# Half-width block products and a spread-out unit order in the feed-forward part of a two-layer encoder trunk

## The chip, the cores and the metric

The kernel runs on one core of one Trainium2 chip. The metric is the time of one execution in microseconds (us) on the device. TensorE (PE) multiplies matrices, VectorE (DVE) and ScalarE (ACT) work element by element, GpSimd (POOL) and SyncE (SP) issue transfers here. Each engine takes its own instructions strictly in the order in which the program lists them for it.

## The reference

Two layers, 256 tokens, width 2048. Each layer is a combined projection, an attention group and a retention group, an output projection, a layer norm, a SwiGLU feed-forward part of width 5632, and a second layer norm. What the change touches is the feed-forward part:

```python
D_MODEL, SEQ, DEPTH, D_FF = 2048, 256, 2, 5632
for l in range(DEPTH):
    ...
    x = layer_norm(ALPHA * x + mix, ln1_g[l], ln1_b[l])
    f = (jax.nn.silu(x @ w_gate[l]) * (x @ w_up[l])) @ w_down[l]
    x = layer_norm(ALPHA * x + f, ln2_g[l], ln2_b[l])
```

All inputs and the output are float32.

## The kernel before

**Units.** All weights reach the chip as blocks of 1 MB (128 partitions x 2048 float32). A list made at build time, `UNITS`, gives the order in which the kernel consumes them, one *unit* at a time. Each unit is prepared in `Weights._prep`: its block is loaded (`raw`), ScalarE rounds it to a high part (`hi`, the cast of L288) and VectorE subtracts to get the low part (`lo`, L289). TensorE then makes three matmuls for each piece: high weights by high activations, low by high, high by low. Three pairs of `hi`/`lo` buffers go round, so that unit number i can be prepared only when TensorE has finished unit i-3; until then the unit has no buffer. Loads are asked for up to four units ahead. This is the heart of `_prep` for a Strassen unit:

```python
if frm is not None and kind not in by_dma:
    V.tensor_tensor(r[into], r[into], r[frm], ALU.add)
split(hi[:, o:o + 2048], lo[:, o:o + 2048], r[into])
```

`split` is the cast and the subtraction. Plain ("std") blocks have long been split in two halves of 1024 columns, a cast and a subtraction each; Strassen units are split in one piece of 2048.

**The feed-forward part.** The first 512 columns of gate and up are computed plainly. The other ten column groups pair the gate and the up projection in a Strassen-Winograd scheme over four weight blocks 11, 12, 21, 22. It needs seven products: B11, B21 and B22 use a block as it is; T1 uses 11+12, T2 uses 11+12+22, T3 uses 12+22, and T4 takes 21 in as well. Here the sums are made in place in `raw`. Most are VectorE additions (L220): T1 and T2 in every group, T3 in half groups too. T4, and T3 in full groups, get their sum by a transfer that POOL issues and that adds into `raw` as it lands (`ADD_BY_DMA`, L225).

**Groups.** A *half* group (`HALF_ORDER`) works on 512 columns and half the depth; four plain units (sg1, sg3, su1, su3) do the rest of the depth. A *full* step is two groups of 256 columns at full depth, and blocks of the down projection (D, `down`) are put between their products (`FULL_ORDER`: four D in a group, or two in the last step). Per layer there are five half groups, eight full groups with four D, and two with two D, in the order half, full, full, half, full, full, and so on; behind them stand the last eight D. In each of the ten Strassen steps, `flush` turns the hidden values of the step before (eight transposes on TensorE, two casts and two subtractions) at a fixed position in the first group.

**Names in rows.** `raw`, `hi`, `lo` are the weight tiles; `sX`, `sY`, `sZ`, `sW`, `sQ`, `sR` are PSUM banks: sX takes B11 and then B21, sW takes T1 and then B22, sY takes T2, sZ takes T3, sQ takes T4, and sX, sQ, sR, sW also take the plain units of a half group; `db` is the bank of a D, `pth` that of the transposes, `v` are the running vectors. L895 is the copy of the B11 result, L916 to L918 finish T4. The build's scheduler arranges each engine's instructions by its own estimate of readiness, so an engine's order can differ from the written one.

Of the kernel before, what the change touches and what calls it, by code (L numbers as in the profile page):

```python
# [13 lines left out]
AF = mybir.ActivationFunctionType  # L14
ALU = mybir.AluOpType
# [5 lines left out]
D = 2048  # L21
# [4 lines left out]
HR = 4  # L26
FF = 5632
NFF = FF // 512
HALF_ORDER = ("B11", "T1", "sg1", "T2", "B21", "sg3", "T3", "su1", "B22", "su3", "T4")
FULL_ORDER = {4: ("B11", "T1", "T2", "D", "B21", "D", "T3", "D", "B22", "D", "T4"),  # L30
              2: ("B11", "T1", "T2", "B21", "D", "T3", "B22", "D", "T4")}
FF_STEPS = [("half", 1, ())]
for _f in (2, 4, 6, 8):
    FF_STEPS += [("full", _f, tuple((n, (_f - 2, _f - 1)) for n in range(4))), ("half", _f + 1, ())]
# [17 lines left out]
def weight_plan():  # L52
# [15 lines left out]
    def strassen(l, c, half=None):  # L68
        rows, nk, c0, ncol = (1024, 4, 512 * c, 512) if half is None else (1024, 8, 512 * c + 256 * half, 256)
        return {i: add("w_gate" if i[1] == "1" else "w_up", l, rows * (int(i[0]) - 1), nk, c0, ncol)  # L70
                for i in ("11", "12", "22", "21")}

    for l in range(DEPTH):
# [28 lines left out]
        for mode, c, groups in FF_STEPS:  # L102
            if mode == "half":
                b = strassen(l, c)
                for kind in HALF_ORDER:
                    if kind[0] == "s":
# [3 lines left out]
            else:  # L110
                todo = [(n, cc) for n, cs in groups for cc in cs]
                per = len(todo) // 2
                for half in range(2):
                    b = strassen(l, c, half)
                    for kind in FULL_ORDER[per]:
                        if kind == "D":
# [12 lines left out]
def shift(b):  # L129
    name, _, _, _, c0, ncol = PLAN[b]  # L130
    if name in ("w_gate", "w_up") and ncol == 256:
        return 48
    if name == "w_in" and ncol == 128 or name in ("w_uq", "w_ukv") and c0 < 1024:
        return 16
    return 0
# [9 lines left out]
def trunk(ctx: ExitStack, tc: tile.TileContext, x, pos, w, lnp, cols, eye, consts, out):  # L145
    nc = tc.nc
    V, A, PE, G = nc.vector, nc.scalar, nc.tensor, nc.gpsimd
# [21 lines left out]
    def bank(tag_name):  # L169
        return psp.tile([P, 512], F32, tag="ps", name=tag_name)  # L170

    class Weights:
# [26 lines left out]
        def _prep(self):  # L199
            i = self.n_prep  # L200
            if i >= len(UNITS):
                return
            self.loads(i + 1)
            hi = wspl.tile([P, W_SPL], F32R, tag="hi", name=f"hi{i}")
            lo = wspl.tile([P, W_SPL], F32R, tag="lo", name=f"lo{i}")
            kind, b = UNITS[i]
            if kind == "std":
                n = SIZES[b]
                raw = self.raw.pop(b)
                o = shift(b)  # L210
                for a, e in ((0, n // 2), (n // 2, n)):
                    split(hi[:, o + a:o + e], lo[:, o + a:o + e], raw[:, a:e])
            else:
                r = {j: self.raw.get(b[j]) for j in b}
                ncol, o = PLAN[b["11"]][5], shift(b["11"])
                by_dma = ADD_BY_DMA[ncol]
                into, frm = {"B11": ("11", None), "B21": ("21", None), "B22": ("22", None), "T1": ("11", "12"),
                             "T2": ("11", "22"), "T4": ("11", "21"), "T3": ("12", "22")}[kind]
                if frm is not None and kind not in by_dma:
                    V.tensor_tensor(r[into], r[into], r[frm], ALU.add)  # L220
                split(hi[:, o:o + 2048], lo[:, o:o + 2048], r[into])
                nxt = {"T1": ("T3", "12", "22"), "T2": ("T4", "11", "21")}.get(kind)
                if nxt is not None and nxt[0] in by_dma:
                    j = b[nxt[2]]
                    G.dma_start(r[nxt[1]], w[OFFS[j]:OFFS[j + 1]].rearrange("(p n) -> p n", p=P), accum_op=ALU.add)  # L225
                for j in {"T4": ("11",), "T3": ("12",), "B22": ("22",), "B21": ("21",)}.get(kind, ()):
                    self.raw.pop(b[j])
            self.hi[i], self.lo[i] = hi, lo
            self.n_prep += 1
            self.loads(i + 4)  # L230
# [56 lines left out]
    def split(hi, lo, src):  # L287
        A.copy(hi, src)  # L288
        V.tensor_tensor(lo, src, hi.bitcast(F32), ALU.subtract)  # L289

    def rsqrt(v, n):
        r = small.tile([P, 4], F32, tag="rs", name="rs")
        G.tensor_tensor(r[:, :n], v, mhalf[:, :n], ALU.pow)
        return r
# [164 lines left out]
    for l in range(DEPTH):  # L459
# [22 lines left out]
        for t in range(2):  # L482
# [7 lines left out]
            r = rsqrt(v, 2)  # L490
# [373 lines left out]
        def xs(t, k0, nk):  # L864
            ts = slice(t * P, (t + 1) * P)
            return (xTh[:, k0:k0 + nk, ts], xTl[:, k0:k0 + nk, ts])

        def mm(ps, unit, st, first=False):
            wh, wl = unit
            nk = st[0].shape[1]  # L870
            for k in range(nk):
                a, b = st[0][:, k, :], st[1][:, k, :]
                PE.matmul(ps, a, wh[:, k, :], start=first and k == 0, stop=False, skip_group_check=True)  # L873
                PE.matmul(ps, a, wl[:, k, :], start=False, stop=False, skip_group_check=True)  # L874
                PE.matmul(ps, b, wh[:, k, :], start=False, stop=k == nk - 1, skip_group_check=True)  # L875

        def strassen_group(order, nk, ncol, c0, v, downs):
            v2, v3, v5, sg = (t[:, c0:c0 + ncol] for t in v)
            s1, s2, s3, s4 = ((sfh[:, i, :nk], sfl[:, i, :nk]) for i in range(4))
            B = {}  # L880

            def acc(name, unit, st):
                new = name not in B
                if new:
                    B[name] = bank("s" + name)[:, :ncol]
                mm(B[name], unit, st, new)

            for i, kind in enumerate(order):
                if kind == "D":
                    next(downs)()  # L890
                    continue
                (unit,) = W.get()
                if kind == "B11":
                    acc("X", unit, xs(0, 0, nk))
                    A.copy(v2, B["X"])  # L895
                elif kind == "T1":
                    acc("W", unit, s1)
                elif kind == "T2":
                    acc("Y", unit, s2)
                    V.tensor_tensor(v2, B["Y"], v2, ALU.subtract)  # L900
                elif kind == "B21":
                    acc("X", unit, xs(0, 8, nk))
                    if "sg3" not in order:
                        A.activation(sg, B["X"], AF.Silu)
                elif kind == "T3":
                    acc("Z", unit, s3)
                    V.tensor_tensor(v3, B["Z"], v2, ALU.add)
                    V.tensor_tensor(v5, B["W"], v3, ALU.add)
                elif kind == "B22":
                    acc("W", unit, s4)  # L910
                    if "su3" not in order:
                        V.tensor_tensor(v2, B["W"], v2, ALU.add)
                        V.tensor_tensor(v2, v2, sg, ALU.mult)
                elif kind == "T4":
                    acc("Q", unit, xs(1, 8, nk))
                    V.tensor_tensor(v3, B["Q"], v3, ALU.subtract)  # L916
                    A.activation(v3, v3, AF.Silu)
                    V.tensor_tensor(v5, v5, v3, ALU.mult)  # L918
                elif kind in ("sg1", "sg3"):
                    acc("X", unit, xs(0, 4 * int(kind[2]), 4))  # L920
                    if kind == "sg3":
                        A.activation(sg, B["X"], AF.Silu)
                    acc("Q", unit, xs(1, 4 * int(kind[2]), 4))
                else:
                    acc("R", unit, xs(1, 4 * int(kind[2]), 4))
                    if kind == "su3":
                        V.tensor_tensor(v5, B["R"], v5, ALU.add)
                    acc("W", unit, xs(0, 4 * int(kind[2]), 4))
                    if kind == "su3":
                        V.tensor_tensor(v2, B["W"], v2, ALU.add)  # L930
                        V.tensor_tensor(v2, v2, sg, ALU.mult)
                W.done()
                if i == 1:
                    flush()

        plain_group()
        for mode, c, groups in FF_STEPS:
            v = [vt512(n) for n in ("v2", "v3", "v5", "sg")]
            if mode == "half":
                strassen_group(HALF_ORDER, 4, 512, 0, v, None)  # L940
            else:
                downs = down_list(groups)
                per = sum(len(cs) for _, cs in groups) // 2
                for half in range(2):
                    strassen_group(FULL_ORDER[per], 8, 256, 256 * half, v, downs)
            hprev.append((c, (v[0], v[2])))
# [124 lines left out]
```

## Time and profile before

| | before |
|---|---|
| median of 3 runs | 2330.65 us (2329.36 to 2331.11) |
| the profiled execution | 2328.0 us, span 2326.2 us |
| PE busy | 2208.3 us, 95% of the span, 12676 matmuls |
| DVE busy | 1696.3 us, 73% |
| ACT busy | 1082.2 us, 47% |
| mean granted clock of TensorE | 0.983 |
| HBM traffic | 202 GB/s over the span |

The span runs from the first to the last instruction of the profiled execution; the time of that execution is a little longer. The ends of matmuls are modelled, so a busy PE is not a PE at its peak; what a stretch costs is better read from the starts of matmuls.

### The profile page before, as it was taken

The numbers are of one execution on the slowest core, as the hardware profiler recorded it, in microseconds if no ns is written. First come the engines' busy times: TensorE is split into PE (matmuls) and PEld (weight loads), VectorE is DVE, ScalarE is ACT, GpSimd is POOL, SyncE is SP. The second block draws the span as 40 slices with busy tenths as digits, with TensorE's granted clock in tenths as the row PEclk, the third lists the DMA queues.
The fourth block names the chain that finished last, engine by engine and source line by source line (L and its number), as shares of the span: only waits on it lengthen the run. The fifth ranks groups of instructions, "written<-read, shape, count | busy, mean of one in ns | idle before, by whom it ended". The sixth has DMA issues, their size and how long they took to land.

```text
span 2326.2 us, 30343 instructions
## 1 busy us (share of the span) xinstructions
PE 2208.3 (95%) x12676; PEld 1929.0 (83%) x12676; DVE 1696.3 (73%) x1795; ACT 1082.2 (47%) x1117; POOL 61.7 (3%) x76
## 2 busy tenths in 40 slices
PE   7999999999999999998999999999999998999998
PEld 6989987878788887887889899878877878888786
DVE  8565676877868777787775656677877787777877
ACT  4554333554545445445345533345454444544542
POOL 0000000000000000000000000000000000000000
PEclk9999999999999999999999999999999999999999
DMA  7544554576676667766654344555657756676573
GB/s 261 199 147 162 177 202 167 201 258 207 188 238 227 216 192 224 236 216 191 225 185 181 145 165 178 206 203 207 207 193 243 240 195 198 228 249 202 188 227 145
DMA packets 67801, 472.37 MB, mean 203 GB/s; under 512 B 7888, under 2 KB 8144, under 8 KB 11984
## 3 DMA queue, kind: packets, MB, share of 16 engines
q1 hardware_dynamic: 60320, 417.94, 47.4%
q0 software_dynamic: 7200, 52.43, 12.3%
q8 instruction: 99, 1.62, 0.3%
q14 instruction: 38, 0.31, 0.0%
q10 hardware_dynamic: 144, 0.07, 0.0%
HBM read 468.31 MB, written 2.10 MB: 202 GB/s over the span
## 4 chain that ended last, share of the span: by engine, by line
PE 38%; DVE 7%; ACT 3%; issue 2%; DMA 0%; DVEq 0%; ACTq 0%
DVE lo L289 3%; PE db L278 3%; PE db L277 3%; PE db L276 3%; ACT hi L288 3%; DVE raw L220 2%; PE prq L284 1%; PE prq L283 1%; PE prq L285 1%; PE sX L873 1%; PE sX L874 1%; PE sX L875 1%; PE wo L278 1%; PE wo L276 1%; PE wo L277 1%
## 5 line engine op out<-in xcount | busy, mean ns | idle before, releaser
L289 DVE TENSOR_TENSOR lo<-raw,hi 128x1024 fp32r<-128x1024 f32 (+3 forms) x744 | 1098.1, 1509 | 465.7 <-ACT hi L288 464.9
L288 ACT CAST hi<-raw 128x1024 fp32r<-128x1024 f32 (+3 forms) x744 | 922.0, 1281 | 1029.7 <-DVE raw L220 230.9
L276 PE MATMUL db<-hi,hTh 128*128 128x512 f32 x704 | 274.2, 393 | 9.0 <-ACT hi L288 9.0
L277 PE MATMUL db<-lo,hTh 128*128 128x512 f32 x704 | 274.3, 390 | 0.0
L278 PE MATMUL db<-hi,hTl 128*128 128x512 f32 x704 | 274.3, 390 | 0.0
L873 PE MATMUL sX<-hi,xTh 128*128 128x256 f32 (+1 forms) x480 | 155.4, 324 | 11.2 <-ACT hi L288 11.2
L276 PEld LDWEIGHTS db<-hi,hTh 128*128 128x128 f32 x704 | 131.3, 188 | 36.1 <-ACT hi L288 12.2
L220 DVE TENSOR_TENSOR raw<-raw,raw 128x2048 f32<-128x2048 f32 x70 | 159.8, 2283 | 0.9 <-DMA raw<-w 0.9
L278 PEld LDWEIGHTS db<-hi,hTl 128*128 128x128 f32 x704 | 132.4, 188 | 26.8
L874 PE MATMUL sX<-lo,xTh 128*128 128x256 f32 (+1 forms) x480 | 153.3, 319 | 0.0
L277 PEld LDWEIGHTS db<-lo,hTh 128*128 128x128 f32 x704 | 132.5, 188 | 24.5
L875 PE MATMUL sX<-hi,xTl 128*128 128x256 f32 (+1 forms) x480 | 152.5, 318 | 0.0
L283 PE MATMUL prq<-xTh,hi 128*128 128x256 f32 x512 | 144.3, 282 | 0.0
L874 PE MATMUL sW<-lo,sfh 128*128 128x256 f32 (+1 forms) x400 | 123.4, 308 | 20.7 <-DVE lo L289 20.7
L284 PE MATMUL prq<-xTl,hi 128*128 128x256 f32 x512 | 142.9, 279 | 0.0
L285 PE MATMUL prq<-xTh,lo 128*128 128x256 f32 x512 | 142.9, 279 | 0.0
L873 PE MATMUL sW<-hi,sfh 128*128 128x256 f32 (+1 forms) x400 | 121.0, 302 | 0.0
L875 PE MATMUL sW<-hi,sfl 128*128 128x256 f32 (+1 forms) x400 | 120.5, 301 | 0.0
L873 PEld LDWEIGHTS sX<-hi,xTh 128*128 128x128 f32 x480 | 90.7, 189 | 22.0 <-ACT hi L288 15.4
L873 PE MATMUL sY<-hi,sfh 128*128 128x256 f32 (+1 forms) x200 | 74.3, 372 | 30.6 <-ACT hi L288 30.6
L874 PEld LDWEIGHTS sW<-lo,sfh 128*128 128x128 f32 x400 | 75.2, 188 | 31.2 <-DVE lo L289 27.7
L283 PEld LDWEIGHTS prq<-xTh,hi 128*128 128x128 f32 x512 | 97.5, 190 | 0.1
(269 smaller groups left out, 4503.5 us busy)
## 6 DMA issues: line engine op xcount, KB each, us to landing
raw<-w SPq DMA_DIRECT2D x377, 1024.0 KB, 5.5
raw<-w POOLq DMA_DIRECT2D x50, 1024.0 KB, 8.9
raw<-w SPq DMA_DIRECT2D x8, 640.0 KB, 3.8
lng<-lnp SPq DMA_DIRECT2D x4, 1024.0 KB, 4.8
lnb<-lnp SPq DMA_DIRECT2D x4, 1024.0 KB, 6.8
res<-x SPq DMA_DIRECT2D x4, 512.0 KB, 6.2
out<-res SPq DMA_DIRECT2D x8, 256.0 KB, 2.3
cst<-consts SPq DMA_DIRECT2D x2, 720.5 KB, 7.8
```

The lines of the kernel that those rows point to most:

```text
L220: V.tensor_tensor(r[into], r[into], r[frm], ALU.add)
L276: PE.matmul(ps[:, :ncol], sh, wh[:, k, :ncol], start=first and k == 0, stop=False)
L277: PE.matmul(ps[:, :ncol], sh, wl[:, k, :ncol], start=False, stop=False)
L278: PE.matmul(ps[:, :ncol], sl, wh[:, k, :ncol], start=False, stop=last and k == nk - 1)
L283: PE.matmul(ps_ap, wh[:, k, c0:c0 + P], xh[:, k, :], start=k == 0, stop=False)
L284: PE.matmul(ps_ap, wh[:, k, c0:c0 + P], xl[:, k, :], start=False, stop=False)
L285: PE.matmul(ps_ap, wl[:, k, c0:c0 + P], xh[:, k, :], start=False, stop=k == nk - 1)
L288: A.copy(hi, src)
L289: V.tensor_tensor(lo, src, hi.bitcast(F32), ALU.subtract)
L873: PE.matmul(ps, a, wh[:, k, :], start=first and k == 0, stop=False, skip_group_check=True)
L874: PE.matmul(ps, a, wl[:, k, :], start=False, stop=False, skip_group_check=True)
L875: PE.matmul(ps, b, wh[:, k, :], start=False, stop=k == nk - 1, skip_group_check=True)
```

## The change

Sums, casts and subtractions of Strassen units go in two halves of 1024 columns. The order of units in a group is another: in full groups a D follows B11, and T1 and T2 no longer follow each other; in half groups T1 and T2 each have a plain unit ahead. The two accumulations of sg1 and sg3 change places (sQ before sX), the Silu of the gate now always stands at B21, and `flush` is called behind unit 2 instead of unit 1.

```diff
-HALF_ORDER = ("B11", "T1", "sg1", "T2", "B21", "sg3", "T3", "su1", "B22", "su3", "T4")
-FULL_ORDER = {4: ("B11", "T1", "T2", "D", "B21", "D", "T3", "D", "B22", "D", "T4"),
-              2: ("B11", "T1", "T2", "B21", "D", "T3", "B22", "D", "T4")}
+HALF_ORDER = ("B11", "sg1", "T1", "sg3", "T2", "B21", "T3", "su1", "B22", "su3", "T4")
+FULL_ORDER = {4: ("B11", "D", "T1", "B21", "D", "T2", "D", "T3", "B22", "D", "T4"),
+              2: ("B11", "D", "T1", "B21", "T2", "D", "T3", "B22", "T4")}
...
-                    V.tensor_tensor(r[into], r[into], r[frm], ALU.add)
-                split(hi[:, o:o + 2048], lo[:, o:o + 2048], r[into])
+                    for e in (0, 1024):
+                        t = r[into][:, e:e + 1024]
+                        V.tensor_tensor(t, t, r[frm][:, e:e + 1024], ALU.add)
+                for e in (0, 1024):
+                    split(hi[:, o + e:o + e + 1024], lo[:, o + e:o + e + 1024], r[into][:, e:e + 1024])
...
-                    if "sg3" not in order:
-                        A.activation(sg, B["X"], AF.Silu)
+                    A.activation(sg, B["X"], AF.Silu)
...
+                    acc("Q", unit, xs(1, 4 * int(kind[2]), 4))
                     acc("X", unit, xs(0, 4 * int(kind[2]), 4))
-                    if kind == "sg3":
-                        A.activation(sg, B["X"], AF.Silu)
-                    acc("Q", unit, xs(1, 4 * int(kind[2]), 4))
...
-                if i == 1:
+                if i == 2:
                     flush()
```

The rows below are what the program lists for an engine, as built, at three places. In all three the place is the start of the second group of the first full step (layer 0); the changed kernel's line numbers are three higher from there on, and the numbers behind names tell tiles apart.

On PE before, where T1 (sW) ends and T2 (sY) begins:

```order
L875 MATMUL sW<-hi_4530,sfl 128x256
L873 MATMUL sY<-hi_4566,sfh 128x256
L276 MATMUL db_4669<-hi_4600,hTh_3948 128x512
L276 MATMUL db_4670<-hi_4600,hTh_3948 128x512
L874 MATMUL sY<-lo_4567,sfh 128x256
L875 MATMUL sY<-hi_4566,sfl 128x256
```

And now, where T2 (sY) begins, behind a D (db):

```order
L279 MATMUL db_4647<-hi_4672,hTh_4321 128x512
L280 MATMUL db_4647<-lo_4673,hTh_4321 128x512
L281 MATMUL db_4647<-hi_4672,hTl_4322 128x512
L876 MATMUL sY<-hi_4703,sfh 128x256
L877 MATMUL sY<-lo_4704,sfh 128x256
L878 MATMUL sY<-hi_4703,sfl 128x256
```

T2 moved from behind T1 to behind a whole D, and no matmul of another unit stands inside it any more.

On DVE before, from the subtraction of the group's B11 on (raw_4403 is block 11, which takes 12 = raw_4438 for T1 and 22 = raw_4470 for T2; raw_4502 is the first D, raw_4536 B21):

```order
L289 TENSOR_TENSOR lo_4499<-raw_4403,hi_4498 128x2048
L731 SCALAR_TENSOR_TENSOR res<-res,db_4440 128x512
L220 TENSOR_TENSOR raw_4403<-raw_4403,raw_4438 128x2048
L731 SCALAR_TENSOR_TENSOR res<-res,db_4441 128x512
L916 TENSOR_TENSOR v_4196<-sQ,v_4196 128x256
L289 TENSOR_TENSOR lo_4531<-raw_4403,hi_4530 128x2048
L918 TENSOR_TENSOR v_4197<-v_4197,v_4196 128x256
L220 TENSOR_TENSOR raw_4403<-raw_4403,raw_4470 128x2048
L289 TENSOR_TENSOR lo_4567<-raw_4403,hi_4566 128x2048
L289 TENSOR_TENSOR lo_4601<-raw_4502,hi_4600 128x1024 x2
```

And now (raw_4434 is block 11, raw_4503 is 12, raw_4610 is 22; raw_4468 is the D behind B11, raw_4537 B21, raw_4571 the second D):

```order
L292 TENSOR_TENSOR lo_4532<-raw_4434,hi_4531 128x1024 x2
L734 SCALAR_TENSOR_TENSOR res<-res,db_4436 128x512
L734 SCALAR_TENSOR_TENSOR res<-res,db_4437 128x512
L222 TENSOR_TENSOR raw_4434<-raw_4434,raw_4503 128x1024
L292 TENSOR_TENSOR lo_4566<-raw_4468,hi_4565 128x1024 x2
L918 TENSOR_TENSOR v_4218<-sQ,v_4218 128x256
L222 TENSOR_TENSOR raw_4434<-raw_4434,raw_4503 128x1024
L920 TENSOR_TENSOR v_4219<-v_4219,v_4218 128x256
L292 TENSOR_TENSOR lo_4602<-raw_4434,hi_4601 128x1024 x2
L292 TENSOR_TENSOR lo_4639<-raw_4537,hi_4638 128x1024 x2
L222 TENSOR_TENSOR raw_4434<-raw_4434,raw_4610 128x1024 x2
L292 TENSOR_TENSOR lo_4673<-raw_4571,hi_4672 128x1024 x2
```

Between the sum of T1 and the sum of T2 now stand the subtractions of T1 and B21; the first half of T1's sum stands ahead of the subtraction of the D.

On ACT before, the same place:

```order
L288 CAST hi_4530<-raw_4403 128x2048
L917 ACTIVATE v_4196<-v_4196 128x256
L895 COPY v_4195<-sX 128x256
L288 CAST hi_4566<-raw_4403 128x2048
L288 CAST hi_4600<-raw_4502 128x1024 x2
```

And now:

```order
L291 CAST hi_4565<-raw_4468 128x1024 x2
L291 CAST hi_4601<-raw_4434 128x1024
L919 ACTIVATE v_4218<-v_4218 128x256
L898 COPY v_4217<-sX 128x256
L291 CAST hi_4601<-raw_4434 128x1024
L291 CAST hi_4638<-raw_4537 128x1024 x2
L291 CAST hi_4672<-raw_4571 128x1024 x2
```

The second half of T1's cast (hi_4601) now stands behind the copy of B11's result from sX, which can run only when TensorE has finished B11.

## Rows read from the trace of the kernel before

**Rows 1.** Windows of both Strassen stretches: length, busy us (instructions) per engine, PEclk, DMA.
```profile
442.70:1123.88 681.18, 639.00 (x3526) 552.99 (x3524) 523.41 (x420) 338.17 (x283) 22.03 (x25) 0.97 0.67 216
1593.06:2270.91 677.85, 634.46 (x3525) 548.81 (x3524) 523.25 (x420) 338.04 (x283) 21.71 (x25) 0.98 0.67 217
```

**Rows 2.** Timeline of PE: start, us, instruction. A D, T4, the next B11; transposes.
```profile
806.44 0.39 PE L276 MATMUL db<-hi,hTh 128*128 128x512 f32 x1
...
811.88 0.28 PE L873 MATMUL sQ<-hi,xTh 128*128 128x256 f32 x1
...
814.71 0.28 PE L873 MATMUL sX<-hi,xTh 128*128 128x256 f32 x1
...
1598.50 1.03 PE L819 MATMUL pth<-ident,sg 128*128 128x128 f32 x8
1599.29 0.48 PE L873 MATMUL sX<-hi,xTh 128*128 128x512 f32 x1
```

**Rows 3.** Windows of single groups in layer 1: full, full, half, last full.
```profile
1635.47:1682.79 47.32, 43.35 (x274) 38.56 (x273) 37.07 (x32) 24.15 (x21) 1.77 (x3) 1.00 0.70 222
1682.79:1729.92 47.13, 43.87 (x267) 39.16 (x265) 34.48 (x28) 22.09 (x19) 1.69 (x2) 0.96 0.71 224
1729.92:1774.80 44.88, 42.94 (x190) 34.37 (x189) 35.95 (x27) 22.99 (x20) 0.88 (x1) 1.00 0.61 211
...
2231.44:2270.91 39.47, 34.69 (x218) 31.64 (x217) 28.83 (x25) 20.18 (x17) 1.73 (x2) 0.91 0.64 189
```

**Rows 4.** Waits of PE over the span: total us, times, longest.
```profile
PE sY L873 <- ACT hi L288: 30.6, 20, 1.6
PE sW L874 <- DVE lo L289: 20.7, 21, 1.8
```

**Rows 5.** Timeline of DVE at the start of a full group, layer 1.
```profile
1683.96 2.29 DVE L289 TENSOR_TENSOR lo<-raw,hi 128x2048 fp32r<-128x2048 f32 x1 [0.55 <-ACT hi L288]
...
1686.50 2.28 DVE L220 TENSOR_TENSOR raw<-raw,raw 128x2048 f32<-128x2048 f32 x1
1690.81 6.76 DVE L289 TENSOR_TENSOR lo<-raw,hi 128x2048 fp32r<-128x2048 f32 x4 [2.02 <-ACT hi L288]
...
1698.58 2.36 DVE L289 TENSOR_TENSOR lo<-raw,hi 128x1024 fp32r<-128x1024 f32 x2 [0.66 <-ACT hi L288]
```

**Rows 6.** Timeline of ACT in the same group.
```profile
1682.02 1.90 ACT L288 CAST hi<-raw 128x2048 fp32r<-128x2048 f32 x1 [5.40 <-DVE raw L220]
...
1685.81 0.37 ACT L895 COPY v<-sX 128x256 f32<-128x256 f32 x1 [1.57 <-PE sX L875]
1688.88 5.60 ACT L288 CAST hi<-raw 128x2048 fp32r<-128x2048 f32 x4 [2.70 <-DVE raw L220]
1697.49 2.00 ACT L288 CAST hi<-raw 128x1024 fp32r<-128x1024 f32 x2 [3.01 <-PE sY L875]
```

**Rows 7.** Timeline of PE where T2 begins in that group.
```profile
1690.83 0.38 PE L873 MATMUL sY<-hi,sfh 128*128 128x256 f32 x1 [1.63 <-ACT hi L288]
1691.78 0.73 PE L276 MATMUL db<-hi,hTh 128*128 128x512 f32 x2 [0.56 <-ACT hi L288]
1693.16 0.58 PE L874 MATMUL sY<-lo,sfh 128*128 128x256 f32 x1 [0.65 <-DVE lo L289]
```

**Rows 8.** Window of the rest of that T2: PEclk is the third number from the end.
```profile
1693.16:1697.29 4.13, 4.13 (x24) 4.13 (x24) 4.13 (x3) 1.31 (x1) 0.86 (x1) 0.63 0.63 93
```

**Rows 9.** DMA issues: line, count, KB each, median us from issue to landing.
```profile
raw<-w SPq DMA_DIRECT2D x377, 1024.0 KB, 5.5
raw<-w POOLq DMA_DIRECT2D x50, 1024.0 KB, 8.9
```

**Rows 10.** Timeline of DVE, then of PE, in a half group around su3 (sR).
```profile
1620.07 0.68 DVE L907 TENSOR_TENSOR v<-sZ,v 128x512 f32<-128x512 f32 x1
1620.67 1.22 DVE L289 TENSOR_TENSOR lo<-raw,hi 128x1024 fp32r<-128x1024 f32 x1
...
1621.94 0.50 PE L874 MATMUL sR<-lo,xTh 128*128 128x512 f32 x1 [0.40 <-DVE lo L289]
```

## The prediction

> **What bounds the kernel now.** I began with the windows over the two Strassen stretches, from the first B11 of a layer to the end of its last T4, since every edit lies in them. They last 681.18 and 677.85 us, 1359.03 together [rows 1]. TensorE is the busiest engine there, but is it at its own pace? The starts of matmuls tell. A D (24 matmuls of 512 columns) runs from 806.44 to 811.88, 0.2267 us a matmul; a T4 (24 of 256 columns) from 811.88 to 814.71, 0.118 each; the eight transposes of a flush take 0.79 us [rows 2]. The written order gives the count: a half group has 7 x 12 + 4 x 24 = 180 matmuls of 512 columns, 40.81 us; a full group with four D has 7 x 24 of 256 and 96 of 512 columns, 19.77 + 21.76 = 41.53 us; one with two D takes 19.77 + 10.88 = 30.65 us. With five, eight and two of them and ten flushes, a layer needs 204.1 + 332.2 + 61.3 + 7.9 = 605.5 us. Two layers need 1211.0, so 1359.0 - 1211.0 = 148.0 us of the stretches are TensorE out of work or slow. That is all that this change can win there.
>
> Where does it sit? Single groups show it: the first group of a full step takes 47.32 us against 42.3 with its flush, the second 47.13 against 41.5, a half group 44.88 against 41.6, the last full group 39.47 against 30.65 [rows 3]. The waits of TensorE name T2 first (sY, waiting for a cast, one wait of up to 1.6 us in each full group) and then T1 (sW, waiting for a subtraction) [rows 4]. Read the group at 1682.79. A unit gets buffers when the unit three places before it is done on TensorE. T1 follows B11 directly, so it has one product of 2.83 us between its buffer and its start, and T2 the same. VectorE subtracts T1 from 1683.96, sums T2 from 1686.50 and can subtract it only from 1690.81; its cast stands between, from 1688.88 [rows 5, 6]. Sum, cast and subtraction of one piece of 2048 columns are 2.28 + 1.90 + 2.29 = 6.5 us in series, for two units on end, against 2.83 us of cover each. TensorE then starts T2 at 1690.83 after 1.63 us of waiting, does two matmuls of the next D and stands again until 1693.16 [rows 7]. Behind that pause T2's 24 matmuls take 4.13 us instead of 2.7, at a mean granted clock of 0.63 [rows 8]: part of it runs at 1.2 GHz instead of 2.4. So a pause is paid again in the clock, and taking it away returns both.
>
> **What the change does, part by part.**
>
> *Order of full groups.* T1 now stands behind B11 and a D, T2 behind B21 and a D (in the last step, behind B21 alone). The buffers of T1 come free when the previous T4 ends, call it 0; T1 starts at 2.83 + 5.44 = 8.27 us. T2's come free when T1 ends at 11.1, and T2 starts at 11.1 + 2.83 + 5.44 = 19.4. Cover for each: 8.27 us instead of 2.83. In a group with two D, T2's buffers come at 8.27, and it starts at 13.9: 5.66 us. Next the work to be covered, with halves. I have no row of a sum of 1024 columns; I bound it by half of 2.28, 1.14, and by the pair of subtractions of 1024, 2.36 / 2 = 1.18 [rows 5], and take the pair, the same operation on the same memory. A pair of casts of 1024 takes 2.00 [rows 6]. Two half sums 2.36, then a cast of the second half 1.0 and its subtraction 1.2: 4.6 us in all, 3.5 to the first half that TensorE can use. That fits into all three covers, with 1.1 us or more left, even if nothing is done ahead of the buffers.
>
> Is it delayed in the queues? The listed orders show two places. On ScalarE the second cast of T1 stands behind the copy out of sX, hence behind the end of B11 at 2.83: 2.83 + 0.37 + 1.0 = 4.2 us. On VectorE one B21 subtraction can come between the two of T1: 4.2 + 1.2 + 1.2 = 6.6 us, 1.7 before T1 starts, and its second half is wanted 1.4 us later still. At T2 the flush stands in the queue of both engines with two casts and two subtractions of 512 columns, 0.6 to 0.7 each by the like-sized 0.68 [rows 10]; T2 has 8.27 us, so it bears 1.4 us. The D behind the flush is tighter: its second operand is the flush's own result. I allow 0.3 us for it in each of the eight first groups of steps with four D.
>
> *Order of half groups.* T1's cover becomes 2.72 + 5.44 = 8.16 us, T2's (buffers when sg1 ends) 2.72 + 0.79 + 5.44 = 8.95, T3's (buffers when sg3 ends, starts after T2 and B21) 5.44. All hold the 4.6. What stays is su3: its first low half must wait for a vector operation of 0.68 that stands ahead of it on VectorE, and TensorE waits 0.40 in the middle of sR [rows 10]. The listed order still has that operation there, so I leave about 0.7 us in each of ten half groups.
>
> *Halves elsewhere.* B11, B21, B22, T3 and T4 get their first half after 1.0 + 1.2 us instead of 1.9 + 2.3. The cost is instructions: 210 splits and 70 sums each become two. A pair costs 2.36 - 2.29 = 0.07 more on VectorE and 2.00 - 1.90 = 0.10 more on ScalarE, so (210 + 70) x 0.07 = 20 us and 21 us over the kernel. The cover is idle time: VectorE is busy 523 of a stretch's 678 us, ScalarE 338 [rows 1], and would be busy 533 of about 612 us and 348. Without the cover it would cost those 20 us. On this the Trainium skill speaks against the change: VectorE: DVE Perf Modes, section "The TRN2 errata", says that each VectorE or ScalarE operation from SBUF pays a fixed latency, so one large tile pays once and many small ones each time. The trace agrees in direction, with 0.07 and 0.10 us a pair at this size; by the rule as by the rows it is engine time off TensorE's path. The same section gives float32 additions of two tensors as (N + 151) / 0.96 ns, an estimate of 1.22 us for a sum of 1024 alone; two of these in series would make the 4.6 us 4.7.
>
> *Transfers.* T3's accumulating transfer starts when T1's sum is done, about 3 us, and lands some 0.9 + 8.9 later [rows 8, 9], at 13; T3's buffers come at 19.4. T4's starts when T2 is subtracted: at about 16 in a group with four D, landing at 26, with buffers at 30.5; at about 13 in one with two D, landing at 23, wanted at 27.8. The latter is the tightest, 4.8 us less a half cast and subtraction. Plain loads land in 5.5. Traffic per group is unchanged; 217 GB/s [rows 1] becomes 217 x 678 / 612 = 240, and the window with the most in rows 3 had 224 over a whole group. I count nothing for it.
>
> **Sum.** Of 148.0 us there stay 10 x 0.7 = 7 for su3, 8 x 0.3 = 2.4 at the flush, and about 3 for starts of matmuls behind transposes (0.1 in each of 30 groups): 12. The gain is 136 us. Against the profiled execution: span 2326.2 - 136 = 2190, its time 2328.0 - 136 = 2192. The median lies 2.65 us above that execution, so the prediction is 2330.65 - 136 = 2194.65, about **2195 us**, 5.8% less.
>
> **Rivals.**
>
> *The stall moves into the queues.* VectorE and ScalarE take instructions in order, and the new order mixes units: a half cast behind the copy from sX, a half sum ahead of the D's subtraction. In the group at 1682.79 the two products B11 and T1 take 8.04 us up to the start of T2 at 1690.83 [rows 3, 7], 2.4 more than their 2 x 2.83. If each of the 20 full groups still lost that, it would be 48 us: 2195 + 48 = 2243. For it: the orders listed. Against it: 1.7 us of slack in my working, and idle time on both engines.
>
> *VectorE becomes the bound in half groups.* T2, B21 and T3 now stand in a row, 2.72 us each, and each wants 2.36 us of VectorE beside evictions of 0.68 [rows 10]. A lag of 1 to 2 us in ten half groups is 10 to 20 us: 2205 to 2215. Against it: T3's sum needs no buffer of `hi` and `lo` and can run during sg3.
>
> *Slower.* The first half sum of T1 stands ahead of the D's subtraction on VectorE. If block 12 has not landed, everything behind it waits, the D first and TensorE with it. 12 takes the place of 22, free when B22 is split, at about 26 of a group's 41.5 us; it lands at 31.5 and is wanted some 2 us before the group's end, at 39.5: 8 us to spare. It decides when loads come more than 8 us later than the median; to cost more than the gain, 136 / 30 = 4.5 us in each group, they must be 12.5 us late; at 13 us late, 0.5 x 30 = 15 over, 2345 us. Against it: before, a sum waits hardly ever for a load, and 5.5 us would have to be more than tripled.
>
> *Nothing happens*, the same pauses at other units: 2331. Against it: the cover of the two units that wait most has tripled in 16 groups and doubled for T2 in the other four.
>
> **How the numbers follow.** The forecast with its small residues, 2183 (all 148 returned) to 2209, has 0.72. VectorE in half groups, to about 2215, has 0.10; the queues, to 2243, 0.12, half of it below 2230. No change 0.02, slower 0.03, a little 0.01 elsewhere. The range 2183 to 2230 leaves out some 0.12, and 0.06 more if residues I have not seen add up. A difference of 0.2% (4.7 us) is about what a measurement of this kernel can tell from none: faster 0.95, same 0.02, slower 0.03.
>
> **What would show it.** A full group from B11 to B11 in 41.5 to 42.6 us and a half group in 42.4; no wait of TensorE above 1 us for T1 or T2; a granted clock of 1.00 in both stretches; pairs of casts and sums at 2.0 and 2.4 us. I am wrong if sY or sW still wait, or if waits appear at a D, at sZ or at sQ: a D that waits for a subtraction points to the queues, an sQ that waits points to POOL's transfer.

## The result and the profile after

The changed kernel takes 2190.02 us (2188.87 to 2190.36, four runs) against 2330.88 us of the kernel before in the same comparison: ratio 0.9394, 95% interval 0.9378 to 0.9411, 6.1% faster. The forecast was 2195.

The windows of the two Strassen stretches, then a first and a second group of a full step, a half group and the last full group of layer 1 (columns as in [rows 1, 3]):

```profile
442.16:1052.85 610.69, 609.93 (x3526) 535.70 (x3524) 529.81 (x553) 347.86 (x386) 22.00 (x25) 1.00 0.75 237
1521.29:2131.75 610.46, 609.70 (x3525) 535.79 (x3524) 529.90 (x552) 347.67 (x386) 21.68 (x25) 1.00 0.75 237
1563.37:1605.93 42.56, 42.56 (x273) 38.52 (x272) 36.82 (x40) 24.12 (x27) 1.72 (x2) 1.00 0.79 247
1605.93:1647.59 41.66, 41.66 (x267) 37.64 (x265) 35.13 (x38) 22.96 (x25) 1.73 (x2) 1.00 0.80 253
1647.59:1689.66 42.07, 41.99 (x190) 34.53 (x189) 37.64 (x39) 24.37 (x27) 0.88 (x1) 1.00 0.68 225
2100.36:2131.75 31.39, 31.05 (x218) 28.77 (x217) 27.91 (x31) 18.70 (x22) 1.73 (x2) 1.00 0.66 174
```

The stretches shrank from 1359.03 to 610.69 + 610.46 = 1221.15 us, by 137.9; the span shrank by 2326.2 - 2187.1 = 139.1. Of the 148.0 us that TensorE lost there, 1221.15 - 1211.0 = 10.1 are left. The granted clock is 1.00 in every row. In TensorE's list of waits sY and sX, and sW's wait for a subtraction (20.7 us before), are gone; one other wait at sW is left, for a vector operation (v), 0.6 us in all. The engine totals of the page:

```profile
PE 2153.2 (98%) x12676; PEld 1897.0 (87%) x12676; DVE 1714.0 (78%) x2075; ACT 1103.4 (50%) x1327; POOL 61.6 (3%) x76
```

VectorE gained 1714.0 - 1696.3 = 17.7 us of work, ScalarE 1103.4 - 1082.2 = 21.2: the price of more and smaller instructions, almost all of it beside TensorE's work. The start of the group at 1605.93, first VectorE, then ScalarE, answers to [rows 5, 6] (the ScalarE rows begin with the cast of B11):

```profile
1603.99 1.22 DVE L222 TENSOR_TENSOR raw<-raw,raw 128x1024 f32<-128x1024 f32 x1
1605.13 2.35 DVE L292 TENSOR_TENSOR lo<-raw,hi 128x1024 fp32r<-128x1024 f32 x2
1607.40 0.41 DVE L918 TENSOR_TENSOR v<-sQ,v 128x256 f32<-128x256 f32 x1
1607.73 1.21 DVE L222 TENSOR_TENSOR raw<-raw,raw 128x1024 f32<-128x1024 f32 x1
1608.87 0.41 DVE L920 TENSOR_TENSOR v<-v,v 128x256 f32<-128x256 f32 x1
1609.20 4.62 DVE L292 TENSOR_TENSOR lo<-raw,hi 128x1024 fp32r<-128x1024 f32 x4
...
1616.01 4.70 DVE L292 TENSOR_TENSOR lo<-raw,hi 128x1024 fp32r<-128x1024 f32 x4
```
```profile
1599.44 2.00 ACT L291 CAST hi<-raw 128x1024 fp32r<-128x1024 f32 x2 [2.51 <-PE sW L878]
...
1606.18 1.05 ACT L291 CAST hi<-raw 128x1024 fp32r<-128x1024 f32 x1 [0.87 <-PE sQ L878]
1607.85 0.42 ACT L919 ACTIVATE v<-v 128x256 f32<-128x256 f32 x1 [0.62 <-DVE v L918]
1608.96 0.37 ACT L898 COPY v<-sX 128x256 f32<-128x256 f32 x1 [0.69 <-PE sX L878]
1609.23 2.95 ACT L291 CAST hi<-raw 128x1024 fp32r<-128x1024 f32 x3
```

T1's first cast starts at 1606.18, when the previous T4 (sQ) has ended; the second stands behind the copy from sX at 1608.96, and the two T1 subtractions are done by about 1611.5 (the four in one row at 1609.20 are T1's two and B21's two; those at 1616.01 are the second D's two and T2's two). T1 starts on TensorE at 1605.93 + 8.27 = 1614.2: nothing waits. The queue order that the first rival feared is there, and costs nothing.

### The profile page after: what moved, and what is told of

Same layout as the page of the kernel before. It is cut to its first block, busy times and chain, and to the rows that moved or that the text cites. A ratio compares the mean times of both kernels' runs of the same rounds, so it can differ in the third digit from the quotient of the medians.

```text
span 2187.1 us, 30843 instructions
## 1 busy us (share of the span) xinstructions
PE 2153.2 (98%) x12676; PEld 1897.0 (87%) x12676; DVE 1714.0 (78%) x2075; ACT 1103.4 (50%) x1327; POOL 61.6 (3%) x76
## 4 chain that ended last, share of the span: by engine, by line
PE 43%; DVE 4%; issue 1%; DMA 1%; ACT 1%; DVEq 0%; ACTq 0%
PE db L280 3%; PE db L279 3%; PE db L281 3%; DVE lo L292 2%; PE sW L876 2%; PE sX L876 2%; PE sX L878 2%; PE sX L877 2%; PE sW L878 2%; PE sW L877 2%; PE prq L288 1%; PE prq L287 1%; PE prq L286 1%; PE wo L281 1%; PE wo L279 1%; PE wo L280 1%
## 5 line engine op out<-in xcount | busy, mean ns | idle before, releaser
L291 ACT CAST hi<-raw 128x1024 fp32r<-128x1024 f32 (+2 forms) x954 | 948.5, 1042 | 894.0 <-issue 174.4
L292 DVE TENSOR_TENSOR lo<-raw,hi 128x1024 fp32r<-128x1024 f32 (+2 forms) x954 | 1115.6, 1210 | 302.9 <-ACT hi L291 300.6
L222 DVE TENSOR_TENSOR raw<-raw,raw 128x1024 f32<-128x1024 f32 x140 | 167.5, 1215 | 0.0
L878 PEld LDWEIGHTS sX<-hi,xTl 128*128 128x128 f32 x480 | 91.1, 190 | 6.2
L287 PEld LDWEIGHTS prq<-xTl,hi 128*128 128x128 f32 x512 | 96.2, 188 | 0.1
L288 PEld LDWEIGHTS prq<-xTh,lo 128*128 128x128 f32 x512 | 96.1, 188 | 0.0
```

The lines of the kernel that those rows point to most:

```text
L222: V.tensor_tensor(t, t, r[frm][:, e:e + 1024], ALU.add)
L287: PE.matmul(ps_ap, wh[:, k, c0:c0 + P], xl[:, k, :], start=False, stop=False)
L288: PE.matmul(ps_ap, wl[:, k, c0:c0 + P], xh[:, k, :], start=False, stop=k == nk - 1)
```

## The experiments

Two theories stood at first. *A, cover*: the new order gives each sum unit 8 us between its buffers and its start, and that is the gain; halves help a little. *B, granularity*: halves are the gain. Each part was run alone, and in one kind of group alone.

**Halves alone** (old order, old flush):

```diff
-                    V.tensor_tensor(r[into], r[into], r[frm], ALU.add)
-                split(hi[:, o:o + 2048], lo[:, o:o + 2048], r[into])
+                    for e in (0, 1024):
+                        t = r[into][:, e:e + 1024]
+                        V.tensor_tensor(t, t, r[frm][:, e:e + 1024], ALU.add)
+                for e in (0, 1024):
+                    split(hi[:, o + e:o + e + 1024], lo[:, o + e:o + e + 1024], r[into][:, e:e + 1024])
```

> The old order of units and the old flush, but Strassen sums, casts and subtractions in halves. Theory A (cover): what removed the pauses is that a sum unit has 8 us between its buffers and its start instead of 2.8; halves only shorten the chain behind the buffers from 6.5 to 4.6 us (3.5 to the first usable half). T1 and T2 still follow each other, so T2 is still late by some 1.5 us in each of 20 full groups and 1 us in half groups: 30 to 50 us of the 138 come back, 2220 to 2240 us, sY still waits. Theory B (granularity): the gain is that TensorE and ScalarE may start on half a unit; then the halves alone give nearly all of it, 2190 to 2205 us.

Measured 2191.41 us, ratio 0.9398 (0.9384 to 0.9412): all of the gain within what can be told. A fell. Two of its groups, the second of a full step and the first of the last full step (windows), and the start of the first of these on VectorE, with ScalarE's cast of B11:

```profile
1606.67:1648.41 41.74, 41.74 (x266) 37.70 (x265) 34.69 (x38) 22.97 (x25) 1.03 (x2) 1.00 0.80 252
2068.64:2100.76 32.12, 31.89 (x226) 29.50 (x225) 30.43 (x34) 19.01 (x23) 1.74 (x2) 1.00 0.83 258
```
```profile
1602.80 2.35 DVE L222 TENSOR_TENSOR raw<-raw,raw 128x1024 f32<-128x1024 f32 x2
...
1605.66 2.35 DVE L292 TENSOR_TENSOR lo<-raw,hi 128x1024 fp32r<-128x1024 f32 x2
...
1608.27 1.21 DVE L222 TENSOR_TENSOR raw<-raw,raw 128x1024 f32<-128x1024 f32 x1
...
1610.87 6.89 DVE L292 TENSOR_TENSOR lo<-raw,hi 128x1024 fp32r<-128x1024 f32 x6
```
```profile
1598.60 2.00 ACT L291 CAST hi<-raw 128x1024 fp32r<-128x1024 f32 x2 [0.83 <-PE sW L878]
```

T1's subtractions begin at 1605.66, a microsecond before the group's own B11 starts, so T1 already has its buffers there. They cannot come from the end of T4 at 1606.67. T2's sum starts at 1608.27 and its subtraction at 1610.87, in time for a start at 1606.67 + 5.66 = 1612.3.

**Order alone** (changed kernel with whole pieces):

```diff
-                    for e in (0, 1024):
-                        t = r[into][:, e:e + 1024]
-                        V.tensor_tensor(t, t, r[frm][:, e:e + 1024], ALU.add)
-                for e in (0, 1024):
-                    split(hi[:, o + e:o + e + 1024], lo[:, o + e:o + e + 1024], r[into][:, e:e + 1024])
+                    V.tensor_tensor(r[into], r[into], r[frm], ALU.add)
+                split(hi[:, o:o + 2048], lo[:, o:o + 2048], r[into])
```

> The new order of units and the new flush, but sums, casts and subtractions of Strassen units in one piece of 2048 columns. Theory A (cover): 8.2 us of cover hold the 6.5 us chain too, so most of the gain stays: 2195 to 2215 us, with what is lost in the groups with two D, where T2 has 5.7 us of cover, and at su3. Theory B (granularity): most of the gain goes, above 2270 us.

Measured 2213.53 us, ratio 0.9494 (0.9480 to 0.9508), as A said; B as it stood fell too. The waits that are left are su3 (sR) and T4 in the groups with two D (sQ), one of which takes 36.38 us against 31.7 between the same starts in the changed kernel:

```profile
PE sR L874 <- DVE lo L289: 8.8, 10, 0.9
PE sQ L874 <- DVE lo L289: 5.2, 4, 1.9
```
```profile
993.95:1030.33 36.38, 33.64 (x225) 31.14 (x224) 30.84 (x26) 18.67 (x16) 1.75 (x2) 0.95 0.75 231
```

**The order in one kind of group alone**, halves everywhere:

```diff
-HALF_ORDER = ("B11", "sg1", "T1", "sg3", "T2", "B21", "T3", "su1", "B22", "su3", "T4")
+HALF_ORDER = ("B11", "T1", "sg1", "T2", "B21", "sg3", "T3", "su1", "B22", "su3", "T4")
...
```

(and in half groups the two accumulations, the Silu and the flush go back to their old places)

> Halves everywhere, the new order and the new flush in full groups alone; half groups keep the old order. Theory A: half groups of the kernel before lost 2.3 us each, 21 us in ten, and halves take part of it back: 2195 to 2208 us, all of the rest in half groups. Theory B: no difference from the changed kernel, 2190 us within 3.

Measured 2189.61 us, ratio 0.9391 (0.9377 to 0.9405), as B said and below A's range. The converse, the new order in half groups alone:

```diff
-FULL_ORDER = {4: ("B11", "D", "T1", "B21", "D", "T2", "D", "T3", "B22", "D", "T4"),
-              2: ("B11", "D", "T1", "B21", "T2", "D", "T3", "B22", "T4")}
+FULL_ORDER = {4: ("B11", "T1", "T2", "D", "B21", "D", "T3", "D", "B22", "D", "T4"),
+              2: ("B11", "T1", "T2", "B21", "D", "T3", "B22", "D", "T4")}
...
```

(and in full groups the flush goes back to its old place)

> Halves everywhere, the new order and the new flush in half groups alone; full groups keep the old order and the old flush. Theory A: the late T2 of 20 full groups stays, 1.5 us each and the flush that waits in T1, 2215 to 2235 us. Theory B: no difference from the changed kernel, 2190 us within 3.

Measured 2198.02 us, ratio 0.9427 (0.9412 to 0.9443), below what A wanted, but also 5 us above the upper end of B's range. Neither order brings what A promised once pieces are halves. By the starts of B11 a half group takes 42.1 us in the new order and 41.8 in the old one with halves, so the new order of half groups costs 0.3 us each, 3 us in all; the new order of full groups gives about as much back, most of it in the four groups with two D (126.6 us together against 129.1 with halves in the old order).

**What the halves do.** Theory C, formed from these runs: I had counted the old cover wrongly. It is two products, 5.66 us, not one; a chain that fits makes no pause, whichever way it is made to fit. Its rivals: E, halves of the sums count; D, it hurts that two units with a sum follow each other. Casts and subtractions in halves, sums whole (against the kernel before):

```diff
-                split(hi[:, o:o + 2048], lo[:, o:o + 2048], r[into])
+                for e in (0, 1024):
+                    split(hi[:, o + e:o + e + 1024], lo[:, o + e:o + e + 1024], r[into][:, e:e + 1024])
```

> The kernel before, with its order and its flush, and casts and subtractions of Strassen units in halves; the sums stay whole. Theory C (cover, counted anew): in the old order T1's buffers come when the last D but one unit ends and T2's when T4 ends, so each has two products, 5.66 us, ahead of it and not 2.83. A chain that fits into 5.66 us makes no pause, whatever the order. Here the first half is ready after 2.28 + 1.0 + 1.2 = 4.5 us and all after 5.7: nearly no pause, 2190 to 2210 us. Theory E: the halves of the sums are what counts, since they let VectorE put other work between; then 2240 us or more.

Measured 2216.14 us, ratio 0.9504 (0.9490 to 0.9518), 6 us above C's range and well below E's. One wait is left in each full group, T2 for its subtraction, for which C's count (4.5 us against 5.66) has no room; then the cast of B11 and the subtraction of T2 in a group whose B11 starts at 529.91:

```profile
PE sY L875 <- DVE lo L290: 17.5, 20, 0.9
```
```profile
521.85 2.00 ACT L289 CAST hi<-raw 128x1024 fp32r<-128x1024 f32 x2 [0.83 <-PE sW L876]
```
```profile
535.58 6.90 DVE L290 TENSOR_TENSOR lo<-raw,hi 128x1024 fp32r<-128x1024 f32 x6 [0.83 <-ACT hi L289]
```

Sums alone in halves:

```diff
-                    V.tensor_tensor(r[into], r[into], r[frm], ALU.add)
+                    for e in (0, 1024):
+                        t = r[into][:, e:e + 1024]
+                        V.tensor_tensor(t, t, r[frm][:, e:e + 1024], ALU.add)
```

> The kernel before, with its order and its flush, and the sums alone in halves; casts and subtractions of Strassen units stay whole. Theory C: the cast waits for both half sums, the chain is 2.36 + 1.9 + 2.3 = 6.6 us against 5.66, as before: 2320 to 2335 us. Theory E: 2240 us or less.

Measured 2337.34 us, ratio 1.0028 (1.0014 to 1.0041): nothing gained, and a trifle lost, 2 us above C's range. E fell. Splitting this one link shortened nothing: the cast behind it is one piece, and waits for both half sums.

**Neighbours or cover?** Whole pieces and half groups as before, T1 and T2 kept apart by a short product alone:

```diff
-FULL_ORDER = {4: ("B11", "T1", "T2", "D", "B21", "D", "T3", "D", "B22", "D", "T4"),
-              2: ("B11", "T1", "T2", "B21", "D", "T3", "B22", "D", "T4")}
+FULL_ORDER = {4: ("B11", "T1", "B21", "T2", "D", "D", "T3", "D", "B22", "D", "T4"),
+              2: ("B11", "T1", "B21", "T2", "D", "T3", "B22", "D", "T4")}
```

> The kernel before, all in whole pieces, half groups and flush as they were; in full groups B21 stands between T1 and T2 and the D's stand behind T2 (B11, T1, B21, T2, D, D, T3, ...; with two D: B11, T1, B21, T2, D, T3, ...), so no two units with a sum follow each other, but each has two short products ahead, 5.66 us, against a chain of 6.5. Theory C: pauses stay in full groups, 2 to 4 us in each, and 2.3 in half groups: 2250 to 2300 us, sY and sW wait. Theory D (neighbours): what pauses TensorE is that two units with a sum follow each other; then only half groups pause: 2205 to 2225 us.

Measured 2305.06 us, ratio 0.9886 (0.9870 to 0.9903). No two sums follow each other, and the pauses stay, 5 us above C's range in the sum. A second group of a full step (window), TensorE's waits in it, and the cast of B11 and the subtraction of T2:

```profile
533.93:581.83 47.90, 45.21 (x267) 40.32 (x265) 34.80 (x29) 21.88 (x19) 1.41 (x2) 0.93 0.71 220
```
```profile
537.45 0.39 PE L874 MATMUL sW<-lo,sfh 128*128 128x256 f32 x1 [0.42 <-DVE lo L289]
...
544.18 0.38 PE L873 MATMUL sY<-hi,sfh 128*128 128x256 f32 x1 [1.12 <-ACT hi L288]
545.12 0.79 PE L276 MATMUL db<-hi,hTh 128*128 128x512 f32 x2 [0.56 <-ACT hi L288]
...
546.50 0.58 PE L874 MATMUL sY<-lo,sfh 128*128 128x256 f32 x1 [0.60 <-DVE lo L289]
```
```profile
525.86 1.91 ACT L288 CAST hi<-raw 128x2048 fp32r<-128x2048 f32 x1 [0.92 <-PE sW L875]
```
```profile
544.16 6.83 DVE L289 TENSOR_TENSOR lo<-raw,hi 128x2048 fp32r<-128x2048 f32 x5 [2.02 <-ACT hi L288]
```

The converse, whole pieces, T1 and T2 side by side behind two D:

```diff
-FULL_ORDER = {4: ("B11", "T1", "T2", "D", "B21", "D", "T3", "D", "B22", "D", "T4"),
-              2: ("B11", "T1", "T2", "B21", "D", "T3", "B22", "D", "T4")}
+FULL_ORDER = {4: ("B11", "D", "B21", "D", "T1", "T2", "D", "T3", "B22", "D", "T4"),
+              2: ("B11", "D", "B21", "D", "T1", "T2", "T3", "B22", "T4")}
...
-                if i == 1:
+                if i == (1 if "sg3" in order else 0):
```

> The kernel before, all in whole pieces, half groups as they were; in full groups T1 and T2 follow each other, but behind two D (B11, D, B21, D, T1, T2, D, T3, ...; with two D: B11, D, B21, D, T1, T2, T3, ...), so each has a D and a product ahead, 8.27 us; flush behind B11. Theory C: a chain of 6.5 us fits, no pause for T1 and T2 in full groups; half groups keep their 2.3 us, and T3 behind T2 in groups with two D waits some 2 us for its accumulating transfer: 2205 to 2225 us. Theory D (neighbours): the pauses stay, above 2270 us.

Measured 2284.07 us, ratio 0.9797 (0.9783 to 0.9812), a miss for both in the total. The second group of a full step, where no flush falls, is free of pauses with the two sums side by side:

```profile
531.83:573.50 41.67, 41.67 (x266) 37.55 (x265) 34.64 (x29) 20.22 (x16) 1.75 (x2) 1.00 0.76 253
```

What kept the total up is two other places. In the first group of each full step the flush now comes early and sX (B21) waits for its subtraction; in the groups with two D, T4 (sQ) waits too:

```profile
PE sX L874 <- DVE lo L289: 23.4, 10, 2.3
...
PE sQ L874 <- DVE lo L289: 7.8, 4, 1.9
```

By the starts of B11 the eight first groups with four D take 38 us more together than in the changed kernel, and the four groups with two D 35 us more; C had allowed nothing for the former and some 8 us for the latter. So D falls: side by side, T1 and T2 pause nothing where there is room. C's rule holds at that place, and its total does not, by my placing of the flush and by T4.

**What the order is worth.** If C is right, a longer chain needs the longer cover. In both of these the half casts of T1 and T2 are done three times over, with the same values, first in halves with the old order, then in the changed kernel (the lines added to both):

```diff
+                    if kind in ("T1", "T2"):
+                        for _ in range(2):
+                            A.copy(hi[:, o + e:o + e + 1024], r[into][:, e:e + 1024])
                     split(hi[:, o + e:o + e + 1024], lo[:, o + e:o + e + 1024], r[into][:, e:e + 1024])
```

> Halves in the old order (as in e1), with each half cast of T1 and T2 done three times over, the same values: 2 x 2.0 us more of ScalarE in each of 60 units. The chain of T1 and T2 becomes 2.4 + 6 or so, 8.4 us to the end and 5.4 to the first half; the second half is wanted 1.4 us after the start. Theory C (cover): old cover 5.66 + 1.4 = 7.1 us, so about 1.3 us are missing at each sum unit of a full group, more behind the queue, and the clock on top: 2230 to 2290 us. Theory F: the order gives nothing once pieces are halves, so both long kernels come out alike.

> The changed kernel with the same threefold half casts of T1 and T2. Theory C: cover 8.27 + 1.4 = 9.7 us holds 8.4, so pauses come back only in the groups with two D, where T2 has 5.66: 2193 to 2210 us, at least 25 us below the long kernel of the old order. Theory F: like the long kernel of the old order within 5 us.

Measured 2299.28 us (ratio 0.9869, 0.9856 to 0.9883) in the old order and 2223.33 us (0.9544, 0.9531 to 0.9557) in the new one: against the two kernels without it in the same comparison (2193.29 and 2192.08, below), the same added work costs 106 us or 31. C's ranges were 9 and 13 us too low; F fell. The second group of the first full step in the old order, with the cast of B11 and the subtraction of T2 there; then that group in the new order, and one with two D:

```profile
534.61:581.65 47.04, 43.77 (x266) 39.16 (x265) 36.34 (x38) 30.31 (x34) 0.88 (x1) 0.96 0.70 224
```
```profile
526.55 2.00 ACT L294 CAST hi<-raw 128x1024 fp32r<-128x1024 f32 x2 [0.83 <-PE sW L881]
```
```profile
543.51 6.90 DVE L295 TENSOR_TENSOR lo<-raw,hi 128x1024 fp32r<-128x1024 f32 x6 [2.29 <-ACT hi L294]
```
```profile
529.48:571.13 41.65, 41.65 (x266) 37.63 (x265) 35.23 (x38) 30.42 (x33) 1.75 (x2) 1.00 0.77 253
992.11:1029.73 37.62, 32.10 (x202) 29.11 (x200) 28.29 (x30) 25.46 (x29) 1.75 (x2) 0.91 0.74 220
```

In groups with four D the new order takes the longer chain without a trace. Some 23 of the 31 us sit in the four groups with two D (the last row: 37.62 us against 31.7), more than I allowed: mostly not at T2 but at T4, whose accumulating transfer starts only when T2 is subtracted. POOL, then ScalarE, then TensorE there:

```profile
1010.70 0.88 POOL L231 DMA_DIRECT2D raw<-w  x1 [13.85 <-DVE lo L295]
```
```profile
1022.50 3.89 ACT L294 CAST hi<-raw 128x1024 fp32r<-128x1024 f32 x4 [8.45 <-DMA raw<-w]
```
```profile
1023.60 0.58 PE L879 MATMUL sQ<-hi,xTh 128*128 128x256 f32 x1 [4.23 <-ACT hi L294]
```

**Both and halves alone, once more**, side by side:

> The changed kernel once more, in more rounds, beside the halves alone in the same call. Theory C: halves alone make the chain fit the old cover too, so the order is worth nothing that can be told: 2190 us and a difference below 0.2%.

> Halves alone in the old order once more (as e1), in more rounds. Theory C: 2191 us, within 0.2% of the changed kernel. A rival, that the order adds what the groups with two D show (3 to 4 us, against 3 lost in half groups), gives the same within a us or two.

Measured 2192.08 us (0.9408, 0.9395 to 0.9421) for the changed kernel and 2193.29 us (0.9413, 0.9400 to 0.9426) for halves alone. The two differ by 1.2 us, 0.05%: given halves, the new order cannot be told from the old one. No version tried beats the changed kernel by more than can be told; the one nearest to it is the change with the old half groups (2189.61).

## Why the prediction was right, and where it was not

**The time and the size of the loss** were right: 148.0 us lost before, 12 expected to stay and 10.1 that stayed, a gain of 136 forecast and 137.9 found in the stretches. That number came from TensorE's own pace alone, and needed only that every pause goes. (Seven products of 2.83 us are 19.81 and not 19.77 us; that moves the loss by 0.8 us.) That the residues agree so well is partly luck: they sit elsewhere than forecast, as told below.

**The new covers** were right. T1's first cast in the trace starts when T4 ends, its second behind the copy from sX, and nothing waits; in the long chain T1's casts start at 529.72, when T4 has ended, its last subtraction ends at 537.5, and T1 starts at 537.74 without a wait: 8.27 us are really there.

**The old cover was wrong.** The prediction says that T1 "has one product of 2.83 us between its buffer and its start, and T2 the same". A unit's buffers come from the unit three places before: for T1 that is the D ahead of T4, so T4 and B11 lie between, and for T2 it is T4 itself, so B11 and T1 do: 5.66 us each. [rows 6] showed it, had I looked: the cast of T1 starts at 1682.02, before T4's end at 1682.79. For T2 in the groups with two D the change left the cover at 5.66 us; the prediction had it doubled. Counted so, halves at 4.6 us fit the old cover too, and the run of halves alone brings the whole gain. But the buffers are not what T1 and T2 waited for, as the next paragraph shows. The two parts of the change are substitutes: beside 2332.34 us of the kernel before in their comparison, halves alone give 141 us and the order alone 119; both together give 141 (2330.88 - 2190.02). Taking the order for the cause would have been a story that fits the result.

**What made the old T2 late** is one long chain, and not its own 6.5 us behind its buffers. T1's buffers were free when T4 began, at 1682.79 - 2.83 = 1679.96, T2's at 1682.79; their casts began at 1682.02 and 1688.88, and [rows 6] name the sum (`raw`, L220) as what both waited for. B11, T1 and T2 are made one after the other in place in one `raw` tile, so each sum must wait until the cast and the subtraction ahead of it have read the tile. The chain begins with the cast of B11, which did wait for its buffers (sW is B22, three units before); ScalarE, then VectorE, in the kernel before:

```profile
1674.72 1.91 ACT L288 CAST hi<-raw 128x2048 fp32r<-128x2048 f32 x1 [0.92 <-PE sW L875]
```
```profile
1676.83 2.28 DVE L289 TENSOR_TENSOR lo<-raw,hi 128x2048 fp32r<-128x2048 f32 x1
...
1679.63 2.28 DVE L220 TENSOR_TENSOR raw<-raw,raw 128x2048 f32<-128x2048 f32 x1
```

It goes on in [rows 5, 6]: cast of T1 1682.02, its subtraction 1683.96, sum of T2 1686.50, its cast 1688.88, its subtraction 1690.81 to 1693.1. From 1674.72 that is 18.4 us, of which three casts, three subtractions and two sums are 17.1; other work of VectorE that stands between them and the steps from engine to engine are the remaining 1.3. TensorE without a pause would be at T2 at 1682.79 + 5.66 = 1688.45, so the room is 13.7 us. The same two numbers, from the cast of B11 to the first subtracted piece of T2 (a half where pieces are halves) and to T2's place, from second groups of a full step:

| kernel | chain, us | room, us | the group over its 41.53 us |
|---|---|---|---|
| before | 18.4 | 13.7 | 5.6 |
| halves alone | 13.5 | 13.7 | 0.2 |
| casts and subtractions in halves | 15.0 | 13.7 | 1.2 |
| T1 and T2 apart by B21 | 20.6 | 16.6 | 6.4 |
| halves, threefold casts, old order | 18.2 | 13.7 | 5.5 |
| the changed kernel | 20.1 | 25.9 | 0.1 |

In these six groups TensorE loses time (by the pause and the low clock behind it) where the chain is longer than the room, and hardly any where it is not; this count also has the miss of casts and subtractions in halves, which C's does not. In the changed kernel the chain also waits for the buffers of T1 and T2, and the room holds that. With T1 and T2 apart the chain is longer because VectorE subtracts B21 between T1's subtraction and T2's sum. The table was worked out after the runs, and none gave T2 a tile of its own, which would be the direct trial. In halves the links overlap, and T2's subtraction starts at 1610.87 - 1606.67 = 4.2 us after B11 and not 8.0. By the total, casts and subtractions in halves give 116 us (2331.75 - 2216.14), the sums in halves nothing by themselves, and all three together 141.

**The clock.** Pauses and low clock went together: 1.00 in both stretches now against 0.97 and 0.98. Kernels with pauses show it again, 0.93 in the group of the apart-but-short order. How much of the 148 us was clock alone was not measured by itself.

**Price of halves.** Forecast 20 us on VectorE and 21 on ScalarE, found 17.7 and 21.2, and none of it on TensorE's path. A sum of 1024 columns takes 1215 ns by its group in the trace; the Trainium skill (VectorE: DVE Perf Modes, "The TRN2 errata") gives an estimate of 1.22 us by its formula, and the trace agrees. Its warning about many small tiles holds as engine time and says nothing here about the kernel's time.

**Residues.** su3 was to cost 0.7 us in each half group; it costs less. A half group takes 42.07 us, 0.5 over TensorE's pace of 41.6. (The half group read for the prediction, 44.88 us, was the slowest of the ten before; seven take 43.9 to 44.0 by the starts of B11.) The flush costs about 0.1 us in a first group (42.56 against 42.32 of its own pace, 41.66 against 41.53 in the second), not 0.3. What I had not forecast is 0.7 to 1.1 us in the last full group of each layer.

**The rivals.** The stall in the queues and VectorE as the bound did not come. The late load did not either: plain loads land in 5.1 us, accumulating ones in 8.7, at 237 GB/s (forecast 240). POOL's transfer for T4 in groups with two D, which I called the tightest, is indeed the first to give way in the new order, as the long chain shows.

## What to carry to other kernels

For each unit of a pipeline write down two numbers: the length of the chain that prepares it, and the time that the busiest engine leaves for it. If several units are made in place in one tile they are one chain, counted from the first that has to wait for a buffer; look in the trace at what each link really waited for before the buffers are blamed. Either number can be mended; mending both is paid once. Halving one link may give nothing while its neighbour waits for the whole, and before a part of a change is called the cause, that part and the rest should each be run alone.

## What was unexpected

Halves of the sums alone cost 0.28% (0.14 to 0.41) in place of gaining anything. And adding 2 x 2.0 us of ScalarE work to each of 60 units costs 106 us where the cover is short, but only 31 where it is long, some 23 of these in four of the thirty groups.
